# Dense block of a two-layer diffusion trunk: modulation columns pinned to their place in VectorE's order, one per step of the first product and four per output tile of the second

## The chip, the cores and the metric

The kernel runs on one core of a Trainium2 chip. The metric is the device time of one execution in microseconds (us): 1848.74 us in the median of three runs before the change (1843.4 to 1850.4). The profile comes from one more execution, which took 1841.07 us; the span of its recorded instructions is 1839.3 us.

## What is computed

A two-layer backbone works on 256 latent tokens and 256 context tokens of width 1024. Each layer modulates its input by vectors that come from a conditioning vector `c` (for the latent tokens) and `c_ctx` (for the context tokens):

```python
mx = (silu_c @ w_ada[l] + b_ada[l])[:, None, :]
mc = silu_cc @ w_ada[l] + b_ada[l]
sh1, sc1, ga1, sh2, sc2, ga2 = jnp.split(mx, 6, axis=-1)
...
x = x + ga1 * (o_x @ w_out[l])
...
x = x + ga2 * ffn(_modulate(_rmsnorm(x, g_ffn[l]), sh2, sc2))
```

`w_ada[l]` is 1024 x 6144. In layer 0 the channel mixer `ffn` is a dense SwiGLU, `(silu(h @ w1) * (h @ w3)) @ w2` with an inner width of 2816; in layer 1 it is a top-2-of-8 mixture of experts. The dense block of layer 0 is the place of this change.

## The kernel before, in words

**Layout.** Activations are held transposed: eight tiles `xt[k]` of 128 features x 512 tokens (256 latent, 256 context). Matrix products are made from split operands: a float32 weight tile `raw` (128x1024, 512 KB) is loaded by the SyncE queue (line 94), copied to a rounded part `whi` by ScalarE (line 102), and the rest `wlo = raw - whi` is made by GpSimd or VectorE (line 104); in the dense block `low_every` is 1 and GpSimd makes all of them. `mm3` (lines 134 to 137) then issues three matmuls per 128x128 block. `pump` and `take` keep two split tiles and two raw loads ahead of the product.

**The modulation columns.** The 6144 modulation outputs of a layer are 48 columns of 128. The first 16 of layer 0 are made by TensorE at the start. The other 80 are a list, `columns` (line 206): layer 0's 16 to 47 and layer 1's 0 to 15 for both conditioning vectors (ns = 2), then layer 1's 16 to 47 for the latent tokens alone (ns = 1). `more(n)` (line 210) finishes n loaded columns by `ada` and calls `fetch` (line 217), which keeps two loads of 512 KB under way on the SyncE queue into the two buffers of the tile `ar` (line 221). `ada` (line 224) multiplies the loaded 128x1024 weights by the broadcast conditioning vector `scb` on VectorE with an accumulated output, once per vector (line 227), and adds the bias (line 228). The mixer and the output projection of layer 0 call `more` for 24 columns; 56 are left when the dense block begins.

**The dense block.** `dense` (line 579) first normalises and modulates the input (`modulated`, lines 267 to 280; `shifted`, lines 282 to 289) into `fhh` and `fhl`. The first product has 22 steps (`FJ`); a step makes two 128x512 accumulators of 24 matmuls each in PSUM (`acc`, three buffers in all), then ScalarE takes the silu of the first (line 594), VectorE multiplies it by the second (line 595), and `cut` splits the result into `gh[j]` (ScalarE, line 151) and `gl[j]` (VectorE, line 152). Each step ends with `more(2)` (line 597). The second product has eight output tiles of 66 matmuls from three weight chunks each; a tile ends with `more(2)` (line 607), the gated addition to `xt` in two halves (VectorE, line 610) and the running sum of squares (`add_sq`, line 237). The sum after the last tile feeds the normalisation of layer 1.

**What sets the order.** The program text gives each engine a sequence, but a list scheduler reorders it when the kernel is built: it goes through the program with its own estimates of durations and gives each engine the earliest instruction in the text that is ready by those estimates. On the chip each engine and each DMA queue then runs its fixed order. An instruction of a column whose load has landed by the estimates can so move ahead of earlier work that is not ready yet. `keep_in_program_order(i)`, which the change calls, adds an edge of order alone from the last instruction traced on the same engine to `i`: `i` cannot be issued before that one. It adds no wait on another engine.

Of the kernel before, what the change touches and what calls it, by code (L numbers as in the profile page):

```python
# [13 lines left out]
ALU = mybir.AluOpType  # L14
# [38 lines left out]
def backbone(ctx: ExitStack, tc: tile.TileContext, a: dict, out: bass.AP, dbg=None):  # L53
    nc = tc.nc
    pe, act, dve, pool, sp = nc.tensor, nc.scalar, nc.vector, nc.gpsimd, nc.sync

    def sb(name, side="left"):
        return tc.tile_pool(name=name, bufs=1, side=side, reuse_waits="tile")
# [5 lines left out]
    def acc(w=512):  # L64
        return psp.tile([128, 512], F32, name="acc", bufs=3)[:, :w]
# [7 lines left out]
    mod = [per.tile([128, 48, 2], F32, name=f"mod{l}") for l in range(2)]  # L73
# [10 lines left out]
    def V(l, n, i=0, w=1):  # L84
        o, _ = VEC[n]
        return vec[:, l, o + i:o + i + w]
# [10 lines left out]
    def pump(ready=2):  # L97
        while len(parts) < ready and raws:
            r, n = raws.pop(0)
            hi = stg.tile([128, 1024], F32R, name="whi", bufs=3)  # L100
            lo = stg.tile([128, 1024], F32R, name="wlo", bufs=3)
            act.activation(hi[:, :n], r[:, :n], AF.Copy)  # L102
            low[0] += 1
            (pool if low[0] % low_every == 0 else dve).tensor_sub(lo[:, :n], r[:, :n], hi[:, :n].bitcast(F32))  # L104
            parts.append((hi, lo))
            if todo:
                raws.append(raw(todo.pop(0)))
        while len(raws) < 2 and todo:
            raws.append(raw(todo.pop(0)))

    def take():
        t = parts.pop(0)
        pump()
        return t
# [19 lines left out]
    def mm3(ps, w, x, first, last):  # L134
        pe.matmul(ps, w[0], x[0], start=first, stop=False)  # L135
        pe.matmul(ps, w[0], x[1], start=False, stop=False)  # L136
        pe.matmul(ps, w[1], x[0], start=False, stop=last)  # L137

    def gemm3(n, xh, xl, w):
        ws = [take() for _ in range(n)]  # L140
        ps = [acc(w) for _ in range(n)]
        for k in range(KT):
            c = slice(128 * k, 128 * k + 128)
            for p, (whi, wlo) in zip(ps, ws):
                mm3(p, (whi[:, c], wlo[:, c]), (xh[k][:, :w], xl[k][:, :w]), k == 0, k == KT - 1)
            if k % 4 == 3:
                advance(2.56 * n * w / 512)
        return ps

    def cut(src, hi, lo):  # L150
        act.activation(hi, src, AF.Copy)
        dve.tensor_sub(lo, src, hi.bitcast(F32))

    def table(fn, x):
        act.activation(warm, x[:, 0:1], fn, scale=0.0)
# [54 lines left out]
    def more(n):  # L210

        for _ in range(n):
            if loaded:
                ada(*loaded.pop(0))
            fetch()

    def fetch():
        while columns and len(loaded) < 2:
            l, j, ns = columns.pop(0)
            r = adp.tile([128, D], F32, name="ar", bufs=2)  # L220
            sp.dma_start(r, a["waT"][l, j])
            loaded.append((l, j, ns, r))

    def ada(l, j, ns, r):
        for s in range(ns):
            o = r if s == ns - 1 else per.tile([128, T], F32, name="sq", bufs=2).bitcast(mybir.dt.bfloat16)
            dve.scalar_tensor_tensor(o, r, 1.0, scb[:, s], op0=ALU.mult, op1=ALU.mult, accum_out=mod[l][:, j, s:s + 1])  # L227
        dve.tensor_scalar(mod[l][:, j, :ns], mod[l][:, j, :ns], V(l, "b_ada", j), None, op0=ALU.add)


    def add_sq(sm, k, w):
        if k == 0:
            act.activation(sm[:, :w], xt[0][:, :w], AF.Square)
        else:
            sq = per.tile([128, T], F32, name="sq", bufs=2)
            act.activation(sq[:, :w], xt[k][:, :w], AF.Square)
            dve.tensor_add(sm[:, :w], sm[:, :w], sq[:, :w])
# [29 lines left out]
    def modulated(l, gname, jsh, jsc, tmp, w, sm, emit, then=None, rs=None, nt=3):  # L267
        A = tmp.tile([128, KT, 2], F32, name="A")
        for s in range(w // 256):
            dve.scalar_tensor_tensor(A[:, :, s], mod[l][:, jsc:jsc + KT, s], 1.0, V(l, gname, 0, 8), op0=ALU.add, op1=ALU.mult)  # L270
        if rs is None:
            rs = at_once(inv_rms(sm[:, :w], w, 128, D))
        if then:
            table(then, rs)
        for k in range(KT):
            t = tmp.tile([128, T], F32, name="ht", bufs=nt)
            for s in range(w // 256):
                c = slice(256 * s, 256 * s + 256)
                dve.scalar_tensor_tensor(t[:, c], xt[k][:, c], A[:, k, s:s + 1], rs[:, c], op0=ALU.mult, op1=ALU.mult)
                emit(k, s, c, t, mod[l][:, jsh + k, s:s + 1])  # L280

    def shifted(hh, hl, k, s, c, t, sh):
        hi, lo, t = hh[k][:, c], hl[k][:, c], t[:, c]
        act.activation(hi, t, AF.Identity, bias=sh)  # L284
        if s:
            act.activation(t, t, AF.Identity, bias=sh)
            pool.tensor_sub(lo, t, hi.bitcast(F32))  # L287
        else:
            dve.scalar_tensor_tensor(lo, t, sh, hi.bitcast(F32), op0=ALU.add, op1=ALU.subtract)
# [289 lines left out]
    def dense(sm):  # L579
        fp = ctx2.enter_context(sb("ffn", "right"))  # L580
        gh = [fp.tile([128, T], F32R, name=f"gh{j}") for j in range(FJ)]
        gl = [fp.tile([128, T], F32R, name=f"gl{j}") for j in range(FJ)]
        with sb("fh") as fh:
            hh = [fh.tile([128, T], F32R, name=f"fhh{k}") for k in range(KT)]
            hl = [fh.tile([128, T], F32R, name=f"fhl{k}") for k in range(KT)]

            def emit(k, s, c, t, sh):
                shifted(hh, hl, k, s, c, t, sh)

            modulated(0, "g_ffn", 24, 32, fh, T, sm, emit, AF.Silu, nt=2)  # L590
            for j in range(FJ):
                ps = gemm3(2, hh, hl, T) if j == 0 else [gemm3(1, hh, hl, T)[0] for i in range(2)]
                s = fh.tile([128, T], F32, name="ht", bufs=2)
                act.activation(s, ps[0], AF.Silu)
                dve.tensor_mul(s, s, ps[1])  # L595
                cut(s, gh[j], gl[j])
                more(2)
        sm = per.tile([128, T], F32, name="sm", bufs=2)
        for m in range(KT):
            p = acc()  # L600
            for c0 in range(0, FJ, 8):
                whi, wlo = take()
                for k in range(min(8, FJ - c0)):
                    c = slice(128 * k, 128 * k + 128)
                    j = c0 + k
                    mm3(p, (whi[:, c], wlo[:, c]), (gh[j], gl[j]), j == 0, j == FJ - 1)
            more(2)
            for s in range(2):
                c = slice(256 * s, 256 * s + 256)
                dve.scalar_tensor_tensor(xt[m][:, c], p[:, c], mod[0][:, 40 + m, s:s + 1], xt[m][:, c], op0=ALU.mult, op1=ALU.add)  # L610
            add_sq(sm, m, T)
            if m == 0:
                table(AF.Sqrt, sm)
        return sm
# [720 lines left out]
        for k in range(KT):  # L1335
            (sp if k % 2 else act).dma_start(out[k], xt[k][:, :256])

    low_every, pace = 2, 3.8
    dve.memset(eps, EPS)
    dve.memset(scv, 0.0)  # L1340
    sp.dma_start(cv, a["cv"])
# [9 lines left out]
    scb = scp.tile([128, 2, D], F32, name="scb")  # L1351
# [6 lines left out]
    with ExitStack() as early:  # L1358
        adp = early.enter_context(sb("adp"))
        with sb("wa", "right") as wa:  # L1360
            rs = ada_first()
        pump(0)
        with ExitStack() as ctx2:
            sm = mixer(0, None, None, None, rs)
        if dbg:
            dbg("x_mix0", xt, sp)
        low_every = 1
        with ExitStack() as ctx2:
            sm = dense(sm)
        low_every = 2  # L1370
# [9 lines left out]
    with sb("ol") as opool:  # L1380
# [3 lines left out]
        pace = 1.2  # L1384
# [3 lines left out]
        low_every = 1000  # L1388
# [144 lines left out]
```

## Time and profile before

| | us |
|---|---|
| median of three runs | 1848.74 |
| profiled execution, its time | 1841.07 |
| profiled execution, span of its instructions | 1839.3 |
| TensorE busy | 1643.1 (89% of the span) |
| VectorE busy | 833.4 (45%) |
| ScalarE busy | 571.4 (31%) |
| GpSimd busy | 397.5 (22%) |

The profile's page adds up the whole span. The stages are read from the windows view, which gives the busy time of each engine in a stretch of the span, the TensorE clock that was granted in it (1.00 is full speed) and the share of the DMA engines. The timeline lists instructions by their start, with the idle time of the engine ahead of them and what ended it in brackets. Other times in this document are from the start of the span.

### The profile page before, as it was taken

To read this page: it belongs to the slowest core of one execution; us is meant where nothing else is said; L and a number is where in the kernel's file an instruction comes from. 1 tells how busy PE (TensorE), PEld (TensorE's weight loads), DVE (VectorE), ACT (ScalarE), POOL (GpSimd) and SP (SyncE) were. 2 spreads that over 40 slices of the span, in tenths; PEclk is the share of its full clock that TensorE was granted. 3 is DMA by queue.
4 is the path that set the end of the run, shared out by engine and by line. 5 is a ranking of instruction groups with operands and counts; after the bars stand their busy time and mean duration, and the time that the engine had idled before them with its cause. 6 is when DMAs were issued, how large, how long until landed. Compare 5 with 4: busy or idle time off the path is not lost. (4 is left out here: it accounts for less than half of the span.)

```text
span 1839.3 us, 21892 instructions
## 1 busy us (share of the span) xinstructions
PE 1643.1 (89%) x8330; PEld 1062.3 (58%) x8330; DVE 833.4 (45%) x1336; ACT 571.4 (31%) x922; POOL 397.5 (22%) x210
## 2 busy tenths in 40 slices
PE   5998998988899999998989848999988969989886
PEld 2885576766778887957333335555544347753422
DVE  3678868998832114465011014443442048840101
ACT  3433534122133225454010023443421037730100
POOL 0431015434454444303000001221210014410000
PEclk8999998999999999999999969999998989999999
DMA  7634134566632335234999974888977999979997
GB/s 297 223 104 149 47 115 124 182 211 238 224 123 92 94 98 197 79 140 195 376 419 418 420 294 183 320 343 335 365 291 307 419 378 358 366 280 421 417 420 293
DMA packets 84621, 476.13 MB, mean 259 GB/s; under 512 B 9808, under 2 KB 10832, under 8 KB 41168
## 3 DMA queue, kind: packets, MB, share of 16 engines
q1 hardware_dynamic: 80976, 459.84, 65.0%
q10 hardware_dynamic: 2592, 7.71, 1.2%
q0 software_dynamic: 864, 6.29, 0.9%
q8 instruction: 89, 1.46, 0.3%
q14 instruction: 100, 0.82, 0.1%
HBM read 472.76 MB, written 1.05 MB: 258 GB/s over the span
## 5 line engine op out<-in xcount | busy, mean ns | idle before, releaser
L898 PE MATMUL acc<-slot,xe 128*64 128x512 f32 x1120 | 270.9, 627 | 58.7 <-DMA slot<-in_wm 31.5
L104 POOL TENSOR_TENSOR wlo<-raw,whi 128x1024 fp32r<-128x1024 f32 (+1 forms) x87 | 224.1, 2584 | 454.0 <-ACT whi L102 337.0
L1039 POOL TENSOR_TENSOR wl<-slot,wh 128x1024 fp32r<-128x1024 f32 x42 | 103.6, 2466 | 656.1 <-ACT wh L1037 656.1
L1039 DVE TENSOR_TENSOR wl<-slot,wh 128x1024 fp32r<-128x1024 f32 x126 | 182.1, 1471 | 127.3 <-ACT wh L1037 127.3
L1037 ACT CAST wh<-slot 128x1024 fp32r<-128x1024 f32 x168 | 175.9, 1052 | 119.7 <-PE acc L898 83.2
L898 PEld LDWEIGHTS acc<-slot,xe 128*64 128x64 f32 x1120 | 94.7, 143 | 201.9 <-issue 189.3
L1108 DVE SCALAR_TENSOR_TENSOR sq<-sq,gs,acc 64x512 f32<-64x512 f32 (+1 forms) x53 | 39.8, 750 | 343.5 <-ACT sq L1107 337.5
L102 ACT ACTIVATE whi<-raw 128x1024 fp32r<-128x1024 f32 (+1 forms) x112 | 116.3, 1041 | 214.1 <-PE acc L136 161.4
L135 PE MATMUL acc<-fhh,whi 128*128 128x512 f32 x352 | 141.2, 404 | 29.5 <-DVE ht L595 13.5
L136 PE MATMUL acc<-fhl,whi 128*128 128x512 f32 x352 | 140.8, 401 | 0.2 <-POOL fhl L287 0.2
L137 PE MATMUL acc<-fhh,wlo 128*128 128x512 f32 x352 | 140.3, 400 | 0.0
L227 DVE SCALAR_TENSOR_TENSOR ar<-ar,scb 128x1024 f32<-128x1024 f32 x80 | 129.1, 1613 | 21.0 <-DMA ar<-in_waT 20.1
L898 PE MATMUL acc<-wh,xr 128*128 128x512 f32 x400 | 130.0, 407 | 8.6 <-DVE gs L1012 3.9
L898 PEld LDWEIGHTS acc<-wh,xr 128*128 128x128 f32 x400 | 72.5, 190 | 43.0 <-issue 26.9
L135 PEld LDWEIGHTS acc<-fhh,whi 128*128 128x128 f32 x352 | 68.3, 194 | 48.4 <-issue 31.2
L898 PE MATMUL acc<-wl,xr 128*128 128x512 f32 x200 | 78.9, 395 | 0.0
L136 PEld LDWEIGHTS acc<-fhl,whi 128*128 128x128 f32 x352 | 68.5, 195 | 15.6 <-POOL fhl L287 1.3
L137 PEld LDWEIGHTS acc<-fhh,wlo 128*128 128x128 f32 x352 | 68.4, 194 | 14.7
L135 PE MATMUL acc<-hh,whi 128*128 128x512 f32 (+1 forms) x192 | 70.7, 375 | 6.4 <-ACT hh L284 6.4
L227 DVE SCALAR_TENSOR_TENSOR sq<-ar,scb 128x1024 bf16<-128x1024 f32 x48 | 69.8, 1456 | 10.0 <-DMA ar<-in_waT 9.9
L1107 ACT ACTIVATE sq<-acc 64x512 f32<-64x512 f32 (+1 forms) x56 | 33.1, 590 | 132.3 <-PE acc L898 132.3
L898 PE MATMUL S<-slot,scv 128*64 128x512 f32 x320 | 72.4, 594 | 0.0
(305 smaller groups left out, 2742.6 us busy)
## 6 DMA issues: line engine op xcount, KB each, us to landing
slot<-in_wm SPq DMA_DIRECT2D x330, 1024.0 KB, 14.7
ar<-in_waT SPq DMA_DIRECT2D x80, 512.0 KB, 3.7
raw<-in_w SPq DMA_DIRECT2D x44, 512.0 KB, 4.4
raw<-in_win SPq DMA_DIRECT2D x28, 512.0 KB, 3.6
wa<-in_wa SPq DMA_DIRECT2D x16, 512.0 KB, 7.2
raw<-in_wout SPq DMA_DIRECT2D x16, 512.0 KB, 4.3
raw<-in_w2d SPq DMA_DIRECT2D x16, 512.0 KB, 3.5
slot<-in_wm POOLq DMA_DIRECT2D x6, 1024.0 KB, 11.0
```

The costliest lines, as they stand in the source:

```text
L102: act.activation(hi[:, :n], r[:, :n], AF.Copy)
L104: (pool if low[0] % low_every == 0 else dve).tensor_sub(lo[:, :n], r[:, :n], hi[:, :n].bitcast(F32))
L135: pe.matmul(ps, w[0], x[0], start=first, stop=False)
L136: pe.matmul(ps, w[0], x[1], start=False, stop=False)
L137: pe.matmul(ps, w[1], x[0], start=False, stop=last)
L227: dve.scalar_tensor_tensor(o, r, 1.0, scb[:, s], op0=ALU.mult, op1=ALU.mult, accum_out=mod[l][:, j, s:s + 1])
L898: return pe.matmul(o, l, r, start=first, stop=last_)
L1037: group("act", lambda hi=hi, src=src: act.copy(hi, src), [], [f"hi{r}"], [i])
L1039: group(en, lambda en=en, hi=hi, lo=lo, src=src: eng[en].tensor_sub(lo, src, hi.bitcast(F32)), [f"hi{r}"], [f"lo{r}"], [i])
L1107: group("act", lambda: act.activation(y[P], h1, AF.Silu), [], [hn[0], f"gg{g}"])
L1108: group("dve", lambda: dve.scalar_tensor_tensor(y[:128 - P.start], y[P], gs[P, gc + u:gc + u + 1], h3, op0=ALU.mult, op1=ALU.mult), [f"gs{ ...
```

## The change

Inside the dense block (`pinned` is True only there) each pass of a column (line 227) is tied behind the instruction that was traced before it on VectorE. The 56 columns of the block are dealt out anew in the text: one after each step of the first product, two after steps 0 and 11 (24 in all), and one, two and one after the three weight chunks of an output tile of the second product (32 in all); before, the text had two after each step (44) and two after an output tile until the list was empty (12).

```diff
     def ada(l, j, ns, r):
         for s in range(ns):
             o = r if s == ns - 1 else per.tile([128, T], F32, name="sq", bufs=2).bitcast(mybir.dt.bfloat16)
-            dve.scalar_tensor_tensor(o, r, 1.0, scb[:, s], op0=ALU.mult, op1=ALU.mult, accum_out=mod[l][:, j, s:s + 1])
+            i = dve.scalar_tensor_tensor(o, r, 1.0, scb[:, s], op0=ALU.mult, op1=ALU.mult, accum_out=mod[l][:, j, s:s + 1])
+            if pinned:
+                tc.keep_in_program_order(i)
         dve.tensor_scalar(mod[l][:, j, :ns], mod[l][:, j, :ns], V(l, "b_ada", j), None, op0=ALU.add)
...
                 cut(s, gh[j], gl[j])
-                more(2)
+                more(1 + (j % 11 == 0))
...
                     mm3(p, (whi[:, c], wlo[:, c]), (gh[j], gl[j]), j == 0, j == FJ - 1)
-            more(2)
+                more(1 + (c0 == 8))
...
-    low_every, pace = 2, 3.8
+    low_every, pace, pinned = 2, 3.8, False
...
-        low_every = 1
+        low_every, pinned = 1, True
         with ExitStack() as ctx2:
             sm = dense(sm)
```

## Rows read from the trace of the kernel before

**Rows 1.** The page, part 1: busy us, share of the span, instructions of two engines.
```profile
PE 1643.1 (89%) x8330; PEld 1062.3 (58%) x8330; DVE 833.4 (45%) x1336; ACT 571.4 (31%) x922; POOL 397.5 (22%) x210
```
**Rows 2.** Windows: from:to, length, busy per engine, clock, DMA share, GB/s; four stages.
```profile
307.20:518.90 211.70, 184.83 (x769) 148.82 (x768) 181.77 (x235) 49.95 (x66) 96.82 (x34) 0.96 0.60 206
518.90:573.40 54.50, 54.50 (x242) 45.11 (x242) 15.69 (x10) 15.74 (x20) 23.98 (x10) 1.00 0.32 96
573.50:696.90 123.40, 123.40 (x532) 98.90 (x531) 17.86 (x22) 30.40 (x35) 52.95 (x24) 1.00 0.31 94
...
785.00:1839.30 1054.30, 927.07 (x4892) 503.20 (x4891) 358.45 (x512) 303.95 (x453) 123.35 (x73) 0.95 0.84 338
```
**Rows 3.** Windows of two single steps of the first product, and one output tile.
```profile
355.70:370.80 15.10, 12.72 (x48) 10.04 (x49) 14.22 (x20) 2.98 (x5) 5.77 (x2) 0.89 0.62 208
426.70:440.80 14.10, 12.80 (x48) 10.04 (x49) 10.98 (x14) 2.99 (x5) 5.65 (x2) 0.88 0.64 225
...
604.30:619.70 15.40, 15.40 (x67) 12.34 (x67) 2.44 (x3) 3.60 (x4) 6.62 (x3) 1.00 0.31 94
```
**Rows 4.** Waits, 290 to 575 us: who waited for whom, us in total, times, longest.
```profile
PE acc L135 <- DVE ht L595: 13.5, 6, 2.9
PE acc L135 <- DVE mod L228: 13.3, 5, 4.1
```
**Rows 5.** Groups of VectorE instructions, 290 to 575 us: count | busy, mean ns | idle before.
```profile
L227 DVE SCALAR_TENSOR_TENSOR ar<-ar,scb 128x1024 f32<-128x1024 f32 x55 | 97.6, 1775 | 20.5 <-DMA ar<-in_waT 20.1
```
**Rows 6.** Timeline of one step with four columns: VectorE, GpSimd's splits, the SyncE queue.
```profile
428.25 5.65 POOL L104 TENSOR_TENSOR wlo<-raw,whi 128x1024 fp32r<-128x1024 f32 x2 [8.39 <-ACT whi L102]
...
428.77 2.86 DVE L152 TENSOR_TENSOR gl<-ht,gh 128x512 fp32r<-128x512 f32 x1
...
431.68 3.30 DVE L227 SCALAR_TENSOR_TENSOR ar<-ar,scb 128x1024 f32<-128x1024 f32 x1
...
435.15 1.22 DVE L227 SCALAR_TENSOR_TENSOR ar<-ar,scb 128x1024 f32<-128x1024 f32 x1
...
436.41 3.78 SPq L221 DMA_DIRECT2D ar<-in_waT  x2
436.42 0.21 DVE L228 TENSOR_SCALAR mod<-mod,vec 128x1 f32<-128x1 f32 x1
...
438.60 1.23 DVE L227 SCALAR_TENSOR_TENSOR ar<-ar,scb 128x1024 f32<-128x1024 f32 x1 [1.97 <-DMA ar<-in_waT]
...
440.00 0.68 DVE L595 TENSOR_TENSOR ht<-ht,acc 128x512 f32<-128x512 f32 x1
...
441.45 1.23 DVE L227 SCALAR_TENSOR_TENSOR ar<-ar,scb 128x1024 f32<-128x1024 f32 x1 [0.78 <-DMA ar<-in_waT]
```
**Rows 7.** Timeline of VectorE: the last column, and a step after it.
```profile
509.53 1.23 DVE L227 SCALAR_TENSOR_TENSOR ar<-ar,scb 128x1024 f32<-128x1024 f32 x1 [1.49 <-DMA ar<-in_waT]
...
530.32 0.69 DVE L595 TENSOR_TENSOR ht<-ht,acc 128x512 f32<-128x512 f32 x1 [7.04 <-PE acc L137]
531.71 2.45 DVE L152 TENSOR_TENSOR gl<-ht,gh 128x512 fp32r<-128x512 f32 x1 [0.70 <-ACT gh L151]
```
**Rows 8.** Timeline of VectorE between two output tiles of the second product.
```profile
619.97 0.88 DVE L610 SCALAR_TENSOR_TENSOR xt<-acc,mod,xt 128x256 f32<-128x256 f32 x2 [12.27 <-PE acc L137]
621.54 1.56 DVE L237 TENSOR_TENSOR sm<-sm,sq 128x512 f32<-128x512 f32 x1 [0.70 <-ACT sq L236]
```
**Rows 9.** Timeline at the start of the dense block, all engines.
```profile
289.74 1.12 PE L257 MATMUL S<-cst,rr 128*128 128x128 f32 x4 [0.57 <-DVE rr L248]
...
290.85 1.22 DVE L227 SCALAR_TENSOR_TENSOR ar<-ar,scb 128x1024 f32<-128x1024 f32 x1
...
291.99 1.26 DVE L279 SCALAR_TENSOR_TENSOR ht<-xt,A,S 128x256 f32<-128x256 f32 x3
...
301.81 1.22 DVE L227 SCALAR_TENSOR_TENSOR ar<-ar,scb 128x1024 f32<-128x1024 f32 x1
...
303.69 0.50 PE L136 MATMUL acc<-fhl,whi 128*128 128x512 f32 x1 [0.21 <-POOL fhl L287]
```

## The prediction

> **What bounds the kernel now.** The page's busy shares come first, and mislead: VectorE is busy 45% of the span, TensorE 89% [rows 1]. The windows by stage correct that. In the first product of the dense block, from 307.2 to 518.9 us, VectorE is busy 181.8 of 211.7 us, while TensorE is idle for 26.9 us and has a clock of 0.96; in the 54.5 us that follow, the same product keeps TensorE busy throughout at clock 1.00, with VectorE at 15.7 us [rows 2]. The line between the two is the end of the columns: the last column's pass starts at 509.53, in the middle of the first product, and after it the multiplication of line 595 waits for TensorE, 7.04 us per step [rows 7], where before TensorE waited for VectorE. So the list scheduler has moved all 56 columns, those that the text has in the second product too, to the first 17 steps (55 last passes from 290 us on [rows 5], one just before). The waits view names the same: TensorE's first matmul of an accumulator waits for line 595 or for the bias addition of a column that is just ahead of it (line 228), 26.8 us in 11 times [rows 4]. The reason is the three accumulators: a step needs two, so the second step after j starts when line 595 of j has read its own.
>
> A single step shows why VectorE is late [rows 3, 6]. Between two multiplications it has four columns, 14.1 us long. Two passes take 1.2 us; the one at 431.68 takes 3.30, and the subtraction of line 152 2.86, each beside one of GpSimd's two weight splits, which run from 428.25 to 433.90. Two gaps, 1.97 and 0.78 us, are waits for a column's load at the head of VectorE's queue; over the whole stretch such waits come to 20.1 us ahead of the last passes [rows 5]. The multiplication stands behind all that.
>
> **The change, part by part.** The work stays the same: 56 columns, their loads, 24 of them with two passes.
>
> *First product, steps 2 to 17.* The stretch 307.2 to 518.9 holds 16 steps; the five after it took 54.5 us, 10.9 each [rows 2]. A step afterwards has one column, two passes. VectorE's load per step: line 595 0.69, line 152 up to 2.86, two passes of 1.22 with their reads and the bias addition (1.22 + 1.22 + 0.4), and 2.08 (3.30 less 1.22) if a second split is met: 8.5 us, under 10.9 [rows 6, 7]. The two steps with two columns come to 11.3 at worst, but line 595 may be late by nearly a whole further step before TensorE notices. So 16 x 10.9 = 174.4 replaces 211.7: **37.3 us** gained. Of it 26.9 are TensorE's idle time, and about 10 its lower clock after each wait: the two steps of rows 3 show 0.88 and 0.89, the free ones 1.00. Bounds: nothing if VectorE stays late, 37.3 if never; I take 37.3, because the load per step is nearest to that of the free steps, and VectorE has 2.4 us over.
>
> *Start of the block.* The statistics' transposes end at 290.86, but the first modulated tile starts at 291.99, behind the column pass of 290.85 [rows 9]. Pinned, this pass cannot be there: 1.1 us. More passes of 1.2 us stood among the modulated tiles (one at 301.81), and TensorE waited there for GpSimd [rows 9]. From nothing to 3 us in all; I take **1.5**.
>
> *Second product.* TensorE is busy for all 123.4 us, with VectorE at 17.9 [rows 2]. Into each tile of 15.4 us come four one-pass columns. From the start of a pass to the end of its bias addition is 1.48 (435.15 to 436.63) [rows 6], so 5.9 for four; line 610 and the sum of squares add 0.88 + 1.56 [rows 8]: 8.4. GpSimd makes three splits per tile, 6.62 us [rows 3]; each can hold one pass for 2.08, 6.2 more: 14.6. That is under 15.4, and since one of the three is already in the 1.56, nearer 13.7. Loads: two buffers, and from the issue at 436.41 to the pass at 441.45 5.0 us [rows 6]; the step there got through four columns, two raw loads and its own work in 14.1. The DMA engines carried 225 GB/s in it [rows 3]; four columns of 512 KB and 1.4 MB of weights in 15.4 us are about 230. So the cover holds, narrowly. If it fails for a tile, the next accumulator is free for two tiles more; a lag costs only what is left of it at the end, because layer 1 begins with the sum of squares, behind the last columns in VectorE's order. Bounds: 0 and 3.3, one held pass; I take **1** lost, nearer to 0 because 13.7 leaves 1.7 us.
>
> *Queues.* A column's load on the SyncE queue waits for the pass two columns earlier, and raw weight loads behind it wait too. In the first product this gets rarer; in the second a raw load can be some 5 us late, the time of one column load. Two split tiles and two raw loads stand ahead, each about 5 us of TensorE's work (15.4 over three chunks), so nothing is charged. GpSimd's and ScalarE's orders are untouched.
>
> *How long a held pass waits* is the one place where a page weighs against the change. The 3.30 us pass beside a split shows a hold of 2.08 us, and a split there takes 2.83 (5.65/2) [rows 6]. The Trainium skill, page "SBUF — State Buffer", section "Who interferes with whom", says that a VectorE instruction with two SBUF inputs and a GpSimd instruction that reads SBUF exclude each other, and that the second to issue blocks until the first has finished. By that rule a pass could lose a whole split; three of 2.83 would make the tile 8.4 + 8.5 = 16.9 in place of 14.6, 1.5 over, 12 us of lag at the end, and the time about 1822. The sum goes by the row.
>
> **Sum.** 37.3 + 1.5 - 1 = 37.8. The profiled execution took 1841.1 us, so 1803.3 by its own clockwork. That execution lies 7.7 us under the median of the runs, so against the median the sum gives 1810.9; I write **1810**.
>
> **The rivals.**
> 1. *The second product becomes VectorE's.* If every one of the four columns meets a split: 4 x (1.48 + 2.08) + 0.88 + 1.56 = 16.7 per tile, 1.3 over, 10 us of lag after eight tiles, paid at the end. For it: GpSimd's splits move with the passes. Against: three splits for four columns, and a column that follows another is past the split. Gain 38.8 - 10.4 = 28.4, time about 1820.
> 2. *Slower: the columns of the second product run one by one.* If the SyncE order lets a column's load go out only when the pass before it is done, a column costs 5.0 + 1.4 = 6.4, a tile 4 x 6.4 + 2.4 = 28 us, 12.6 over, 101 us in eight tiles, which the gain of 38.8 doesn't pay: about 1911. The point from which it decides is a tile of 20.2 us (38.8/8 over 15.4), a column period of 4.45. Against: the step of rows 6 has four columns in 14.1 us, other work included.
> 3. *The pin does not act as written.* It names only the last instruction traced ahead; were the later ones free to move before line 595, VectorE would stay late: 1849. Against: each pass is tied, and the bias addition depends on its pass.
> 4. *Given back later.* From 785 us on the DMA engines are busy 84% [rows 2]. If the expert weights were limited by a start that does not move, half could be lost: about 1830. Against: those loads go into buffers that the earlier stages free, so they move along.
>
> **How the numbers follow.** Forecast 0.76, rivals 0.12, 0.04, 0.04, 0.04. No change is what lies within 0.5%, 9.2 us, about what a measurement of this kernel can tell. Faster: forecast, rivals 1 and 4, 0.92; same: 0.04; slower: 0.04. Range: the low end is the largest gain, 37.3 + 3, against the profiled execution, 1800.8, less some 2 us because the runs scatter by 7; the high end, 1831, takes in rivals 1 and 4. That leaves out rivals 2 and 3 and a share of the forecast's scatter.
>
> **What would show it.** Right: windows of the first product at 10.9 per step with clock 1.00 and no wait of line 135 for line 595 or 228; passes of line 227 until the end of the second product; second product at 123 to 125 us; everything behind it the same length. Wrong: a tile of over 15.4 us with line 610 late behind line 227, waits of TensorE for `wlo` in the second product, or columns still gone by the middle of the first.

## The result, and the profile after

The changed kernel took 1805.37 us in the median of four runs (1802.37 to 1807.94), the kernel before 1847.86 beside it (1843.4 to 1850.4). The ratio is 0.9772, 95% interval 0.9747 to 0.9797: faster by 42 us, where 38 were forecast and a time of 1810. In the changed file lines from 228 on stand two lower: 595 of before is 597, 610 is 612, 228 is 230.

The first view is the windows of the changed kernel: the 16 steps that answer to the long window of [rows 2], the five after them, the second product, and the experts' stretch from 88 us behind the dense block on (from:to, length, busy us of TensorE, its weight loads, VectorE, ScalarE, GpSimd, clock, DMA share, GB/s).

```profile
306.70:480.60 173.90, 173.90 (x768) 143.98 (x768) 114.89 (x122) 51.73 (x66) 81.92 (x33) 1.00 0.49 152
480.60:535.00 54.40, 54.40 (x241) 45.05 (x240) 30.95 (x35) 15.74 (x20) 24.09 (x10) 1.00 0.47 142
535.00:658.40 123.40, 123.40 (x530) 98.92 (x529) 69.33 (x125) 30.29 (x34) 54.88 (x24) 1.00 0.70 226
746.70:1806.10 1059.40, 932.74 (x4894) 504.58 (x4892) 358.23 (x512) 304.30 (x453) 123.77 (x74) 0.94 0.83 336
```

The 16 steps went from 211.7 to 173.9 us, TensorE without a gap and at a granted clock of 1.00, the upper of its two levels (2.4 GHz). The second product stays at 123.4 us, although VectorE now works 69.3 us in it and the DMA engines are busy 70% of it, where [rows 2] had 17.9 us and 31%. VectorE's total hardly moves; the page's first line, against [rows 1], says how little such a share tells:

```profile
PE 1639.3 (91%) x8330; PEld 1060.7 (59%) x8330; DVE 824.2 (46%) x1336; ACT 573.4 (32%) x922; POOL 382.2 (21%) x210
```

The waits of TensorE and VectorE around the dense block (who waited for whom, us, times, longest) show the roles exchanged, against [rows 4]: VectorE waits for TensorE before its multiplication (597) and its addition (612), and TensorE's one wait in the two products is ahead of their first matmul, for the first modulated tile.

```profile
PE acc L135 <- ACT fhh L286: 1.7, 1, 1.7
...
DVE ht L597 <- PE acc L137: 65.2, 18, 4.4
DVE ar L227 <- DMA ar<-in_waT: 24.1, 12, 3.3
DVE xt L612 <- PE acc L137: 23.3, 7, 3.6
```

A step of the first product and a tile of the second, from VectorE's timeline (start, us; in brackets the idle time ahead and what ended it):

```profile
502.87 0.69 DVE L597 TENSOR_TENSOR ht<-ht,acc 128x512 f32<-128x512 f32 x1 [4.37 <-PE acc L137]
504.25 2.45 DVE L152 TENSOR_TENSOR gl<-ht,gh 128x512 fp32r<-128x512 f32 x1 [0.70 <-ACT gh L151]
506.63 1.22 DVE L227 SCALAR_TENSOR_TENSOR sq<-ar,scb 128x1024 bf16<-128x1024 f32 x1
...
507.88 1.22 DVE L227 SCALAR_TENSOR_TENSOR ar<-ar,scb 128x1024 f32<-128x1024 f32 x1
...
509.15 2.47 DVE L230 TENSOR_SCALAR mod<-mod,vec 128x2 f32<-128x2 f32 x1
513.75 0.69 DVE L597 TENSOR_TENSOR ht<-ht,acc 128x512 f32<-128x512 f32 x1 [2.13 <-PE acc L137]
...
600.09 1.21 DVE L227 SCALAR_TENSOR_TENSOR ar<-ar,scb 128x1024 f32<-128x1024 f32 x1
...
601.48 1.21 DVE L227 SCALAR_TENSOR_TENSOR ar<-ar,scb 128x1024 f32<-128x1024 f32 x1
...
605.36 1.69 DVE L227 SCALAR_TENSOR_TENSOR ar<-ar,scb 128x1024 f32<-128x1024 f32 x1 [2.41 <-DMA ar<-in_waT]
...
607.36 1.23 DVE L227 SCALAR_TENSOR_TENSOR ar<-ar,scb 128x1024 f32<-128x1024 f32 x1
...
612.43 0.88 DVE L612 SCALAR_TENSOR_TENSOR xt<-acc,mod,xt 128x256 f32<-128x256 f32 x2 [3.59 <-PE acc L137]
```

One column stands between two multiplications where [rows 6] had four, and VectorE still waits 2 to 4 us ahead of the multiplication, in 18 of the 22 steps. In the tile the four columns go in two pairs, with one wait for a load between them, and VectorE is ready for the addition 3.6 us before TensorE is.

### The profile page after: what moved, and what is told of

Read it like the earlier page. It is cut to its first block, busy times and chain, and to the rows that moved or that the text cites. A ratio compares the mean times of both kernels' runs of the same rounds, so it can differ in the third digit from the quotient of the medians.

```text
span 1806.1 us, 21857 instructions
## 1 busy us (share of the span) xinstructions
PE 1639.3 (91%) x8330; PEld 1060.7 (59%) x8330; DVE 824.2 (46%) x1336; ACT 573.4 (32%) x922; POOL 382.2 (21%) x210
## 5 line engine op out<-in xcount | busy, mean ns | idle before, releaser
L104 POOL TENSOR_TENSOR wlo<-raw,whi 128x1024 fp32r<-128x1024 f32 (+1 forms) x87 | 211.8, 2435 | 431.1 <-ACT whi L102 314.0
L135 PE MATMUL acc<-fhh,whi 128*128 128x512 f32 x352 | 137.5, 393 | 1.7 <-ACT fhh L286 1.7
L227 DVE SCALAR_TENSOR_TENSOR ar<-ar,scb 128x1024 f32<-128x1024 f32 x80 | 106.6, 1332 | 25.6 <-DMA ar<-in_waT 24.1
L137 PEld LDWEIGHTS acc<-fhh,wlo 128*128 128x128 f32 x352 | 66.6, 189 | 13.7
```

The costliest lines, as they stand in the source:

```text
L227: i = dve.scalar_tensor_tensor(o, r, 1.0, scb[:, s], op0=ALU.mult, op1=ALU.mult, accum_out=mod[l][:, j, s:s + 1])
```

## The experiments

The theory: TensorE was late because VectorE's fixed order held more work between two multiplications of line 595 than a step of TensorE is long; the pins take the surplus out. Rivals: the number of columns per step in the text is what helps; or any pinned order is good, however full. For the second product the rivals are that its cover is limited by loads, by VectorE instructions held up beside GpSimd's splits, or by nothing.

The table gives all twelve runs. "First" is from the first matmul of the first product to that of the second, "second" from there to the last group of three matmuls, 0.6 us for that group included, "to experts" from that group's start to the first expert matmul, "experts" from there to the end of the span; these four are from one profiled execution each, and "second" and "to experts" share the 0.6 us of that group. Each ratio is to executions of the kernel before that ran beside it.

| kernel | time, us | ratio to before, 95% | first | second | to experts | experts |
|---|---|---|---|---|---|---|
| before | 1847.86 | | 280.1 | 123.1 | 177.0 | 966.2 |
| the change | 1805.37 | 0.9772 (0.9747 to 0.9797) | 242.5 | 123.1 | 177.8 | 970.6 |
| x1: the change again | 1802.37 | 0.9747 (0.9717 to 0.9778) | 241.8 | 123.1 | 176.8 | 964.7 |
| x2: pins only | 1805.89 | 0.9762 (0.9736 to 0.9788) | 243.0 | 123.1 | 176.8 | 970.8 |
| x3: dealt out only | 1849.27 | 0.9991 (0.9975 to 1.0008) | 283.6 | 123.1 | 179.6 | 969.9 |
| x4: three a step | 1823.69 | 0.9864 (0.9836 to 0.9891) | 261.0 | 123.1 | 177.0 | 969.5 |
| y1: six a tile | 1839.50 | 0.9957 (0.9941 to 0.9973) | 242.2 | 144.0 | 192.1 | 968.0 |
| y2: pins in the first product | 1812.45 | 0.9813 (0.9795 to 0.9830) | 242.7 | 129.8 | 177.7 | 966.9 |
| y3: pins everywhere | 1800.18 | 0.9748 (0.9731 to 0.9766) | 242.1 | 123.1 | 175.4 | 967.0 |
| y4: splits on VectorE | 1810.14, one run | | 241.8 | 123.1 | 179.8 | 970.4 |
| z1: y2, squares moved | 1810.00 | 0.9784 (0.9755 to 0.9813) | 242.6 | 125.2 | 179.2 | 968.9 |
| z2: y1, squares moved | 1849.16 | 1.0013 (0.9997 to 1.0030) | 242.7 | 135.0 | 208.5 | 967.9 |
| z3: the change, five rounds | 1806.64 | 0.9766 (0.9743 to 0.9789) | 242.6 | 123.1 | 177.6 | 971.9 |
| z4: y3 once more | 1802.10 | 0.9752 (0.9732 to 0.9773) | 242.3 | 123.1 | 175.4 | 964.8 |

**x1, the change again.** No edit.

> The changed kernel once more. Both theories: about 1805 us, 42 us less than before, no wait of TensorE in the dense block. The stretch from the end of the dense block to the end of the span was 1142.4 us before and 1147.5 in the first profile of the change; if those 5 us are scatter, it lies anywhere between 1140 and 1150 here, if they belong to the change it is 1147 or more again.

The experts' stretch, the same code everywhere, lies between 964.7 and 971.9 us over all profiles; the change itself gave 970.6, 964.7 and 971.9. The 4.4 us that its first profile has more there than that of before (966.2, and 969.9 in x3, which runs the same orders) lie inside that scatter. From the last group on, the two stretches together are 1143.2 us before, 1148.4 in the change's first profile and 1141.5 here.

**x2, pins only.**

```diff
-                more(1 + (j % 11 == 0))
+                more(2)
...
-                more(1 + (c0 == 8))
+            more(2)
```

> Pins as in the change, but two columns after each step of the first product and two after an output tile, as before. Theory (TensorE is late when VectorE's own work between two multiplications exceeds a step of 10.9 us): a step with two two-pass columns has about 10 us, worked out from the 14.2 us that VectorE was busy in a step with seven passes less three passes of 1.25; so between no loss and 1 us in each of the first 12 steps against the change, 1805 to 1817. Rival (the number per step is what helps): near the time before, 1840 to 1850.

The time is that of the change. VectorE's step with two two-pass columns was longer than expected. These are the multiplications at both ends of the first such step and at the end of the twelfth, in VectorE's timeline, and TensorE's wait for this line:

```profile
309.35 0.69 DVE L597 TENSOR_TENSOR ht<-ht,acc 128x512 f32<-128x512 f32 x1 [4.59 <-ACT ht L596]
...
323.40 0.68 DVE L597 TENSOR_TENSOR ht<-ht,acc 128x512 f32<-128x512 f32 x1
...
449.00 0.68 DVE L597 TENSOR_TENSOR ht<-ht,acc 128x512 f32<-128x512 f32 x1
```

```profile
PE acc L135 <- DVE ht L597: 0.2, 1, 0.2
```

The first such step takes 14.05 us, the eleven others 11.42 each, half a microsecond over TensorE's step of 10.9. The twelve take 139.65 us where TensorE needs some 131: a lag of about 9 us. The third accumulator covers nearly a step, and that was used up: TensorE waited for line 597 once, 0.2 us, at the end of the twelve. So the pins are needed; dealing the columns out more thinly is not needed for the time, but it leaves slack.

**x3, dealt out only.**

```diff
-        low_every, pinned = 1, True
+        low_every, pinned = 1, False
```

> The columns dealt out as in the change, one a step and four a tile, but without pins. Theory: the list scheduler floats them forward as before, three to four a step, and the time is that of before, 1843 to 1852, with the last column in the first product. Rival (the number per step in the text is what helps): about 1805.

No difference from before. The reason is exact: without pins the list scheduler gives all five engines the instruction orders of the kernel before, one by one, as the two traces show. The number per step in the text changed nothing that reached the chip. The run is thereby a second profile of the program before, and TensorE's waits in it repeat [rows 4]:

```profile
PE acc L135 <- DVE mod L230: 14.8, 5, 4.4
PE acc L135 <- DVE ht L597: 12.7, 7, 3.3
```

Its first product took 283.6 us against 280.1 in the profile that the prediction read, whose execution was a short one. That is part of why the times differ by 42 us and the stages of the first two profiles by 38.

**x4, three a step.**

```diff
-                more(1 + (j % 11 == 0))
+                more(3)
...
-                more(1 + (c0 == 8))
```

> Pins as in the change, but three columns after each step of the first product until all 56 are done, none in the second. Theory: the first eight steps have six passes each, some 13 to 14 us of VectorE's work against 10.9, so TensorE loses 2 to 3 us in each after the first step's slack of 10.9 is used up, 10 to 20 us with the lower clock that follows waits; the one-pass columns behind them fit, 3 x 1.5 and the rest under 10.9. 1815 to 1825. Rival (a pin is enough, wherever the columns stand): 1805.

As the theory expected; the rival, that a pin is enough, is out. A VectorE step with three two-pass columns takes 14.04 us in the timeline, 3.1 more than TensorE's, and TensorE waits again:

```profile
350.99 0.68 DVE L597 TENSOR_TENSOR ht<-ht,acc 128x512 f32<-128x512 f32 x1
...
365.03 0.68 DVE L597 TENSOR_TENSOR ht<-ht,acc 128x512 f32<-128x512 f32 x1
```

```profile
PE acc L135 <- DVE ht L597: 12.7, 6, 2.9
```

The first product is 18.5 us longer than the change's, the time 18 to 21. The six waits are 12.7 us of it; the rest goes with the clock, of which 0.95 was granted in the mean from 306 to 419.5 us. Twelve steps of 11.42 us just fit into the slack; eight of 14.04 do not.

**y1, six a tile.**

```diff
-                more(1 + (j % 11 == 0))
+                more(j < 8)
...
-                more(1 + (c0 == 8))
+                more(2)
```

> As the change, but the first product makes a column only after its first eight steps and each output tile of the second has six (48 in all, 16 of them with two passes). Theory (the second product is covered only as long as a tile's columns end before the next tile's sums): in the changed kernel's tiles columns come in pairs, some 6.2 us from pair to pair because the next loads go out when the pair is done; three pairs are 18.6 us and with the sums 19 to 20 against 15.4, so some 30 us of lag after eight tiles, of which TensorE sees what is left at the end: 1820 to 1840. Rival (loads don't limit, only VectorE's work does): 6 x 1.5 + 2.4 + 6.2 of holds = 17.6, some 17 us. Second rival (the accumulators hide it all): 1803.

The size fits the theory, the place does not. Only 15 us are paid behind the second product (192.1 against 176.8 to 177.8); 21 us are in it, where the prediction had said that the spare accumulators hide a lag. TensorE did not wait for an accumulator, but for split weights. The waits of TensorE and ScalarE in the second product name the way; TensorE's two come to 14.8 us, and the rest goes with a granted clock of 0.95 in this product:

```profile
PE acc L137 <- POOL wlo L104: 7.6, 4, 2.4
PE acc L135 <- ACT whi L102: 7.2, 2, 4.9
```

```profile
ACT sq L238 <- DVE xt L612: 70.9, 5, 16.4
```

ScalarE makes the square of each finished tile (`add_sq`). It waits there for VectorE's addition, up to 16.4 us, and the weight splits of line 102 stand behind it in its order.

**y2, pins in the first product only.**

```diff
     def dense(sm):
+        nonlocal pinned
...
+        pinned = False
         sm = per.tile([128, T], F32, name="sm", bufs=2)
```

> Columns dealt out as in the change, pinned only in the first product. Theory: the columns share two load buffers in turn, so a free column of the second product cannot load before the pinned ones ahead of it have been worked off; the first product stays at 242 us and the time at 1802 to 1806, with the 32 one-pass columns running at their load rate early in the second product. Rival (the pins of the second product keep its columns from floating back): 32 columns return to the first product, TensorE waits for line 595 again, and the time is 1820 to 1845.

Neither time was met. The first product keeps its 242.7 us, so the theory was right that the columns do not return there; yet the second product is 6.7 us longer. Its 32 columns now run as fast as they load, and the addition of line 614 (612 plus the two added lines) comes late behind them. The timeline of three engines:

```profile
575.13 1.23 DVE L227 SCALAR_TENSOR_TENSOR ar<-ar,scb 128x1024 f32<-128x1024 f32 x1 [1.89 <-DMA ar<-in_waT]
...
576.28 0.87 DVE L614 SCALAR_TENSOR_TENSOR xt<-acc,mod,xt 128x256 f32<-128x256 f32 x2
...
577.19 0.63 ACT L238 ACTIVATE sq<-xt 128x512 f32<-128x512 f32 x1 [8.58 <-DVE xt L614]
577.73 1.04 ACT L102 ACTIVATE whi<-raw 128x1024 fp32r<-128x1024 f32 x1
...
578.85 3.09 POOL L104 TENSOR_TENSOR wlo<-raw,whi 128x1024 fp32r<-128x1024 f32 x1 [7.59 <-ACT whi L102]
```

One late addition on VectorE stops ScalarE for 8.58 us and GpSimd for 7.59, and TensorE waits 6.0 us for `wlo` in all:

```profile
PE acc L137 <- POOL wlo L104: 6.0, 3, 2.3
```

Pinned, each tile's columns go behind the sum of squares of the tile before, and the change has no such wait over 1.6 us.

**z1 and z2, the squares moved.** In both kernels the square is made on VectorE:

```diff
-            add_sq(sm, m, T)
             if m == 0:
+                dve.tensor_mul(sm, xt[m], xt[m])
                 table(AF.Sqrt, sm)
+            else:
+                sq = per.tile([128, T], F32, name="sq", bufs=2)
+                dve.tensor_mul(sq, xt[m], xt[m])
+                dve.tensor_add(sm, sm, sq)
```

> The pins in the first product only, as in the run that took 1812, and the squares of the dense block's output (add_sq, on ScalarE) made by VectorE instead. Theory: there the second product took 129.8 us because ScalarE's square of a tile waits for line 612's addition on VectorE, which is late behind columns, and the weight splits (line 102) stand behind that square in ScalarE's order; with the square gone from ScalarE the second product is back at 123 to 124 us and TensorE waits for no wlo, the time 1803 to 1807. Rival (weights are late because their loads stand behind column loads on the SyncE queue): the 6 us of waits for wlo stay, 1810 to 1814.

The second product goes from 129.8 to 125.2 us and TensorE's waits for `wlo` from 6.0 to 1.6. So most of it was ScalarE's order. For the rest the rival is the likely cause, not a shown one: ScalarE now waits 36.4 us for weight loads, where it waited 6.9 in y2 and not at all in the change. TensorE's wait and those of ScalarE in z1:

```profile
PE acc L137 <- POOL wlo L104: 1.6, 2, 0.8
```

```profile
ACT whi L102 <- PE acc L136: 59.4, 15, 4.8
ACT whi L102 <- DMA raw<-in_w2d: 36.4, 8, 7.8
```

The time did not settle it: 1810.00 against 1812.45 is where the rival expected it, and the run of 1803.92 lies far under its other three. The stage did.

> Six columns a tile, as in the run that took 1839.5 with a second product of 144.0 us, and the squares on VectorE. Theory: without ScalarE's wait TensorE's waits for whi and wlo in the second product fall from 14.8 us to under 4, the product to 123 to 130 us, and VectorE's lag, now with one more operation a tile, is paid at the end, 15 to 35 us behind the last matmul; the sum 1825 to 1840. Rival (the loads on the SyncE queue, which waited 128 us for columns there): the second product stays at 140 to 146.

Here the number was missed: 135.0 us, between the two. TensorE's waits for split weights fell from 14.8 to 8.3 us (6.5 + 1.8), and ScalarE's for loads stand at

```profile
ACT whi L102 <- DMA raw<-in_w2d: 62.3, 11, 9.2
```

With six columns a tile both ways cost: the SyncE queue holds raw loads behind column loads, and those wait for VectorE:

```profile
SPq L221 <- DVE mod L230: 87.4, 26, 5.0
```

The lag at the end grew (208.5 us to the experts, 192.1 in y1). Both stretches together are 7.4 us longer than in y1 and VectorE is busy in them 3.0 us longer, 238.0 us, so its added squares are at most a part of the reason. The kernel is no faster than before.

**y4, splits on VectorE.**

```diff
-        low_every, pinned = 1, True
+        low_every, pinned = 1000, True
```

> As the change, but the weight splits of the dense block (line 104) run on VectorE, so that GpSimd does nothing there behind the first tiles. Theory (a pass of 3.3 us is a pass of 1.22 held up by a split on GpSimd): no pass of line 227 in the dense block is over 1.3 us, line 152 takes 0.69, VectorE's own load per step is 0.7 + 0.7 + 2 x 1.2 + 2.8 = 6.6 us, and TensorE still does not wait: first product 242 us, second 123. Rival (passes are long because of their own operands or of the loads that land meanwhile): passes of over 2 us remain.

As the theory expected: the longest of the 80 passes took 1.227 us, against 3.428 in the change (durations in ns, shortest, median, longest), and TensorE waited no more than there.

```profile
L227 DVE SCALAR_TENSOR_TENSOR ar<-ar,scb x56: 1212/1224/1227, 312.6 to 657.0; 128x1024 f32<-128x1024 f32 x56
...
L227 DVE SCALAR_TENSOR_TENSOR sq<-ar,scb x24: 1215/1218/1221, 311.4 to 537.9; 128x1024 bf16<-128x1024 f32 x24
```

```profile
L227 DVE SCALAR_TENSOR_TENSOR ar<-ar,scb x56: 1210/1225/3299, 314.0 to 653.7; 128x1024 f32<-128x1024 f32 x56
...
L227 DVE SCALAR_TENSOR_TENSOR sq<-ar,scb x24: 1211/1212/3428, 310.5 to 538.5; 128x1024 bf16<-128x1024 f32 x24
```

The second fence is the change. The single time, 1810.14, shows no gain.

**y3, z3 and z4, pins from the first column on.**

```diff
-    low_every, pace, pinned = 2, 3.8, False
+    low_every, pace, pinned = 2, 3.8, True
```

> As the change, and the 24 columns of the mixer and the output projection of layer 0 are pinned too. If those columns delay the mixer's short VectorE instructions as the dense block's did, the start of the first product, 293 us, comes earlier by several us and the time is under 1800; if their place in the text is a bad one (behind a whole projection, ahead of the next softmax), the start comes later by 5 us or more; the theory names no side, since in the mixer TensorE is not kept busy by one long product.

> The changed kernel, to be compared with the next run on the same chip: 1800 to 1807.

> Pins from the first column on, once more beside the changed kernel. If the pins in the layer-0 mixer are worth something, it is 1 to 5 us faster than the run before it; if the 2 us seen so far are scatter, the two agree within 2.

On the same chip 1802.10 stands beside 1806.64, and 1800.18 was seen before; the 4.5 us are what was expected of a real gain, and "to experts" is 175.4 us in both of its profiles, 176.8 to 177.8 in the three of the change. But the intervals of the ratios overlap (0.9752, 0.9732 to 0.9773, beside 0.9766, 0.9743 to 0.9789), and the first product did not start earlier (294.7 us in z4's profile, 293.6 in z3's). It beats the kernel before; that it beats the change is not shown.

## Why the prediction was right

**First product.** The main term was right: 37.3 us forecast for 16 steps, 37.8 in the windows (211.7 less 173.9). Its division holds too: 26.9 us were TensorE's idle time in the 16 steps, and its busy time for the same matmuls fell by the other 10.9 (184.8 to 173.9), with the clock at 1.00 where the mean was 0.96. Over the whole first product its waits fell from 29.6 us (26.8 of [rows 4] and 2.8 for the first tiles) to 1.7. x4 and x2 confirm the reason by its number: the load per step against 10.9 us, with a step of slack.

Two readings behind that term were wrong without harm. The load of 8.5 us is not "nearest to that of the free steps": those have 3.1 (15.69 in five), the step of [rows 3] at 426.70 has 11.0. What carries the term is that 8.5 is under 10.9, and the step shown above took 8.8, from 502.87 to the end of its bias addition at 511.62. The hold that was allowed for a pass came in its bias addition in place of that (2.47 us for 0.23). And "11.3 at worst" for a step with two columns was met by the second of the two such steps (438.00 less 426.71), but not by the first, with 14.06, where two passes and a bias addition were held:

```profile
308.08 0.69 DVE L597 TENSOR_TENSOR ht<-ht,acc 128x512 f32<-128x512 f32 x1 [4.62 <-ACT ht L596]
...
322.14 0.68 DVE L597 TENSOR_TENSOR ht<-ht,acc 128x512 f32<-128x512 f32 x1
```

The slack took that up, as the prediction had said; x2 shows how much of such excess it can take.

**Start.** 1.5 us forecast, 0.9 measured. The time at which the first matmul starts can't tell it: 293.46 before and 292.72 in the change, but 293.0 and 293.6 in x1 and z3, the same program, and 295.6 in x3, the order of before. TensorE's idle time ahead of that matmul can. It is 2.61 us before and 2.62 in x3, 1.71 or 1.72 in x1, x2, z3 and the change; here before and the change:

```profile
293.46 1.65 PE L135 MATMUL acc<-fhh,whi 128*128 128x512 f32 x3 [2.61 <-ACT fhh L284]
```

```profile
292.72 1.65 PE L135 MATMUL acc<-fhh,whi 128*128 128x512 f32 x3 [1.72 <-ACT fhh L286]
```

With the column pass gone, what is late next is the warm-up behind ScalarE's table load; VectorE's first modulated tile in the change waits for it:

```profile
291.24 1.26 DVE L281 SCALAR_TENSOR_TENSOR ht<-xt,A,S 128x256 f32<-128x256 f32 x3 [1.41 <-ACT warm L155]
```

The further passes among the modulated tiles were worth nothing: from the first matmul to the 16 steps it is 13.7 us before and 14.0 in the change, at a mean clock of 0.82 and 0.78.

**Second product.** Forecast: covered, with 1 us lost. Measured: covered, nothing lost. The margin was wider than thought: VectorE was ready 3.6 us before the addition, where 13.7 of 15.4 us leave 1.7, because the holds were over-sized. Up to 6.2 us of them in each tile had been allowed for. In the change's eight tiles six of 33 last passes were held, by 0.4 to 1.1 us; the mean is 1.335 us, 0.11 above an undisturbed one, so 3.7 us in all. The other 27 took at most 1.23, and all but one of them began while no split ran. A held pass waits for what is left of the split: the pass at 605.36 shown above ends at 607.05, 1.08 us after this split does (605.97):

```profile
603.59 2.38 POOL L104 TENSOR_TENSOR wlo<-raw,whi 128x1024 fp32r<-128x1024 f32 x1 [3.96 <-ACT whi L102]
```

So it is with all 239 passes of the dense block that began during a split, in the 13 profiles with splits on GpSimd: they end 1.08 to 1.21 us after the split does. The prediction's dearer reading of the rule (the Trainium skill, "SBUF — State Buffer", "Who interferes with whom"), a whole split lost per pass, was not met. The rule itself, that the later of the two waits until the first has finished, agrees with these ends.

With rival 1 the direction was right and the place wrong: y1 and y2 show that a late addition costs long before the accumulators run out, through ScalarE's order. The step that failed is "a lag costs only what is left of it at the end". It did no harm here because the pins keep the lag at nothing. Rival 2's way, loads on the SyncE queue, shows in z1 and z2, not in the change's order. Rival 3 did not occur: the passes stand where the pins put them, the last at 653.7 us, in the second product. Rival 4 did not: the stretches behind the dense block scatter, and none keeps a gain back.

**The sum.** 37.8 us forecast and 38.3 read between the profiles (the last addition starts at 658.64, before at 696.97). That the sum is so close is partly luck: the start was taken 0.6 too high and the loss in the second product 1 too high. The times show 41 to 46. The profiled execution of before, 1841.07, was shorter than any of its unprofiled ones, and the same order in x3 took 3.5 us more in the first product. What else makes the difference between executions was not tried.

## What to carry to other kernels

Work that is always ready, like weight columns that only wait for a load, is moved forward by a list scheduler into gaps that its estimates show; here that filled an in-order engine ahead of the instruction that another engine waits for (what the estimates were, no run shows). Tie such work to its place, and count the engine's load between two urgent instructions against the length of the step, held instructions included. Spare buffers pay for a few steps of excess and not for many. Before a lag is called free because of them, follow every in-order queue that waits on the late instruction: here one addition on VectorE stopped ScalarE, and with it the weights.

## What the runs showed of the hardware that was not expected

A two-column bias addition (`tensor_scalar`, 128x2, one tensor input) is held up by a GpSimd split like a pass with two tensor inputs: 0.87 us in the mean of 24 in the change, seven of them 2.2 to 2.5, the others 0.23, and never over 0.23 where the splits ran on VectorE (y4). The one-column form, 128x1, took 0.21 in the mean of 32:

```profile
L230 DVE TENSOR_SCALAR mod<-mod,vec 128x2 f32<-128x2 f32 x24 | 20.9, 872 | 0.9
L230 DVE TENSOR_SCALAR mod<-mod,vec 128x1 f32<-128x1 f32 x32 | 6.8, 214 | 1.1
```

That the two forms meet different splits is not the reason. In the 13 profiles with splits on GpSimd 107 of the one-column form began while a split ran, and none took over 0.22 us; 46 of the two-column form did, and each took at least 1.58. One of the 107, inside a split that ends at 560.36:

```profile
557.39 2.97 POOL L104 TENSOR_TENSOR wlo<-raw,whi 128x1024 fp32r<-128x1024 f32 x1 [3.69 <-ACT whi L102]
```

```profile
558.15 0.21 DVE L230 TENSOR_SCALAR mod<-mod,vec 128x1 f32<-128x1 f32 x1
```

This split shows the hold from the other side too: it began during a pass (556.88 to 558.11) and took 2.97 us, where one that meets none takes 2.38.

The Trainium skill, page "SBUF — State Buffer", section "Who interferes with whom", says that `tensor_scalar` can contend with GpSimd when it runs in a two-port mode; the two forms here agree with that, though no run shows the mode itself.
